# Seven-product up projections: h kept in fp32 for its combinations, made in three portions

## The chip, the cores and the metric

The kernel runs on one core of a Trainium2 chip. A core has TensorE (PE in the profile; PEld is its weight load), VectorE (DVE), ScalarE (ACT), GpSimd (POOL) and SyncE (SP), which here only issues transfers. The metric is the device time of one execution in microseconds, lower is better; the runs shown give a median.

## What is computed

A decoder trunk of two layers on 512 tokens of width 1024, all in fp32. Each layer is a half-step FFN, a token mixer and another half-step FFN, and each of the three starts with an adaptive norm:

```python
mod = cond @ ada_w[l] + ada_b[l]          # nine vectors: shift, scale, gate of three sub-layers
h = modulate(x, norm_ffn1[l], sh1, sc1)   # rms_norm(x) * gain * (1 + scale) + shift
x = x + 0.5 * (1.0 + g1)[:, None] * swiglu(h, ffn1_w1[l], ffn1_w3[l], ffn1_w2[l])
# swiglu(h, w1, w3, w2) = (silu(h @ w1) * (h @ w3)) @ w2, hidden width 2816
h = modulate(x, norm_mix[l], sh2, sc2)
x = x + (1.0 + g2)[:, None] * token_mix(h, ...)
h = modulate(x, norm_ffn2[l], sh3, sc3)
x = x + 0.5 * (1.0 + g3)[:, None] * swiglu(h, ffn2_w1[l], ffn2_w3[l], ffn2_w2[l])
```

The change touches the four FFNs (ffn1 and ffn2 of both layers), the norms ahead of them and the work of the conditioning.

## The kernel before

Activations lie feature-major: 128 features by 512 tokens, x as 8 such k-tiles. Every fp32 product is made of three passes over rounded parts: a factor is split into a high part (a cast, ACT) and a low part (value less high part, DVE), and `mm3` multiplies high by high, high by low and low by high. The normed h is kept only in parts, `hhi` and `hlo`. Weights come in slabs of 128 x 1024 (`slab`): SP issues the transfer into a `raw` buffer (there are 2), ACT casts the halves into `whi` (L120), DVE subtracts for `wlo` (L121); there are 3 buffers each of whi and wlo.

An FFN has 22 m-tiles of the hidden width. The first ones (4, or 6 in the very first FFN) are made plainly: `first` (or `first_begun`) and then `up(m)`, each with one slab of w1 and one of w3, and Silu and a product behind (`glu`: ACT L492, DVE L493). The others go in pairs of m-tiles (`pairs`) with seven block products in place of eight. For these h is cut into four blocks of 4 k-tiles by 256 tokens, b11, b12, b21, b22, and `fast_acts` makes four combinations of them, each split again into parts and kept in two tiles with the tag `A`: b11 - b12, then the negative of its sum with b22, then of that with b21, and b22 - b12 apart, which GpSimd computes. Since h is there in parts only, a difference takes three operations of 128 x 1024 and each further sum two; the running results take two of the five `L` buffers. `fast_acts` is called after the first `up(m)`. The pairs load their weight blocks into `raw` and `L`, two of them as a sum, where a second transfer, issued by GpSimd, adds to the first (L538).

After m-tiles 0 to 7, 8 to 15 and 16 to 21 comes a down projection each (`down`, through `close`), whose result is added to x (L388). The third close has more to do: its last four output tiles are made in two halves of 256 tokens, with the weights in the freed `A` tiles (`spare`), so that the norm of the next sub-layer can start on the first half while the second is multiplied. A norm sums squares (ACT L322, DVE L323), sums over partitions with PE, computes the inverse root on DVE, spreads it with PE, and then `norm_apply` makes h k-tile by k-tile: scaled on DVE (L378), high part with the shift on ACT (L379), low part on DVE (L384), or for k = 3, 5, 7 the full h on ACT (L381) and the low part on GpSimd (L382). In the first FFN of layer 0 `begin` does this in an order written out by hand; there L1479 and L1444 make hhi and hlo.

The conditioning (`mod`) is a product of a vector with 72 weight blocks a layer. `ada_block` loads one block of 512 KB into `L` (SP) and makes one DVE operation with it (L268). They wait in a queue, and `tick` takes one or more from it at set places: two after each `up(m)` past the first, two after each pair, one per output tile of a down projection. What is left is emitted by `drain` before the mixer.

The framework's planner puts each engine's instructions into their order: it follows the order of the code, but lets an instruction pass an earlier one that it reckons not ready; only those named to `keep_in_program_order` (the conditioning products, the beginning, the first half's norm on PE) keep theirs. Each engine and each transfer queue then works strictly in its planned order. Buffers are named by tags, with the counts in `BUFS` (`c3` 5, `cv` 3, `g` 7); a tile waits until an older one of its tag is done with.

Of the kernel before, what the change touches and what calls it, by code (L numbers as in the profile page):

```python
# [73 lines left out]
class Trunk:  # L74
    def __init__(self, ctx, tc, aps):
        self.tc = tc
        self.nc = tc.nc
        self.ap = aps
        self.sb = ctx.enter_context(tc.tile_pool(name="sb", bufs=1))
        self.ps = ctx.enter_context(tc.tile_pool(name="ps", bufs=1, space=bass.MemoryType.PSUM))  # L80
        self.count = 0
        self.pin = False
        self.units, self.body, self.ahead = [], None, None
        self.queue = []
        self.waiting = []

    def order(self, i):

        return self.tc.keep_in_program_order(i)
# [20 lines left out]
        return self.ps.tile(list(shape), F32, tag=tag, name=f"{tag}_{self.count}", bufs=BUFS[tag])  # L110


    def slab(self, src, n, place=None):
        nc = self.nc
        raw = self.t("raw", [P, 1024])
        hi, lo = place or (self.t("whi", [P, 1024], F32R), self.t("wlo", [P, 1024], F32R))
        nc.sync.dma_start(raw[:, :n], src)
        for a in range(0, n, 512):
            s = slice(a, min(a + 512, n))
            nc.scalar.copy(hi[:, s], raw[:, s])  # L120
            nc.vector.tensor_sub(lo[:, s], raw[:, s], hi[:, s].bitcast(F32))  # L121
        return hi, lo
# [7 lines left out]
    def split(self, hi, lo, src, scale=None):  # L130

        nc = self.nc
        if scale is None:
            nc.scalar.copy(hi, src)
            nc.vector.tensor_sub(lo, src, hi.bitcast(F32))  # L135
        else:
            nc.scalar.activation(hi, src, AF.Identity, scale=scale)
            nc.vector.scalar_tensor_tensor(lo, src, scale, hi.bitcast(F32), ALU.mult, ALU.subtract)
# [229 lines left out]
    def norm_apply(self, j, gain, mod, cols, rb):  # L368
        nc = self.nc
        a, b = cols  # L370
        if a == 0:
            self.hhi = self.t("hhi", [P, KT, SEQ], F32R)
            self.hlo = self.t("hlo", [P, KT, SEQ], F32R)
        for k in range(KT):
            h = self.t("g", [P, SEQ])
            sh = mod[:, 3 * j * KT + k:3 * j * KT + k + 1]
            hi, lo = self.hhi[:, k, a:b], self.hlo[:, k, a:b]
            nc.vector.scalar_tensor_tensor(h[:, a:b], self.x[:, k, a:b], gain[:, k:k + 1], rb, ALU.mult, ALU.mult)  # L378
            nc.scalar.activation(hi, h[:, a:b], AF.Identity, bias=sh)  # L379
            if k in (3, 5, 7):  # L380
                nc.scalar.activation(h[:, a:b], h[:, a:b], AF.Identity, bias=sh)  # L381
                nc.gpsimd.tensor_sub(lo, h[:, a:b], hi.bitcast(F32))  # L382
            else:
                nc.vector.scalar_tensor_tensor(lo, h[:, a:b], sh, hi.bitcast(F32), ALU.add, ALU.subtract)  # L384

    def residual(self, m, ps, gate, cols):
        a, b = cols
        self.nc.vector.scalar_tensor_tensor(self.x[:, m, a:b], ps[:, a:b], gate[:, m:m + 1], self.x[:, m, a:b],  # L388
                                            ALU.mult, ALU.add)

    def close(self, get, acts, gate, finish, spare=(), ahead=None):

        late = KT - len(spare)
        for m in range(late):
            s = get(m)
            ps = self.p("acc")
            self.proj(ps, s, acts)
            self.residual(m, ps, gate, FULL[0])
            if finish is not None:
                finish(m, FULL[0])  # L400
            self.tick()
        ws = [get(m, place) for m, place in zip(range(late, KT), spare)]
        if ahead is not None:
            ahead()
        self.tick(len(ws))
        norms = []
        for (a, b), tag in zip(HALVES if ws else (), ("acc", "sc")):
            for m, s in zip(range(late, KT), ws):
                ps = self.p(tag)
                n = len(acts)  # L410

                cut = NORM_AT.get(m - late, n) if norms else n
                self.proj(ps, s, acts, (a, b), range(cut))
# [14 lines left out]
        return [self.slab(self.ap[f"{w}_{n}"][l, m].rearrange("p k c -> p (k c)"), 1024)  # L428
                for n, m in (("w1", 0), ("w3", 0), ("w1", 1))]

    def fast_acts(self):


        nc = self.nc

        def quarter(i, j):
            return [t[:, 4 * i:4 * i + 4, j * 256:(j + 1) * 256] for t in (self.hhi, self.hlo)]

        f32 = lambda t: t.bitcast(F32)
        b11, b12, b21, b22 = (quarter(i, j) for i in range(2) for j in range(2))  # L440
        store = [self.t("A", [P, 4, 4, 256], F32R) for _ in range(2)]
        places = [(st[:, i], st[:, i + 1]) for st in store for i in (0, 2)]
        new = lambda: self.t("L", [P, 4, 256])

        def difference(a, b, eng):
            t = new()
            eng.tensor_sub(t, f32(a[0]), f32(b[0]))
            eng.tensor_add(t, t, f32(a[1]))
            eng.tensor_sub(t, t, f32(b[1]))
            return t  # L450

        def minus_sum(a, b):

            nc.vector.scalar_tensor_tensor(a, a, -1.0, f32(b[0]), ALU.mult, ALU.subtract)
            nc.vector.tensor_sub(a, a, f32(b[1]))

        def split(place, t):
            nc.scalar.copy(place[0], t)
            nc.vector.tensor_sub(place[1], t, f32(place[0]))

        t = difference(b11, b12, nc.vector)
        split(places[0], t)
        t3 = difference(b22, b12, nc.gpsimd)
        minus_sum(t, b22)
        split(places[1], t)
        minus_sum(t, b21)
        split(places[3], t)
        split(places[2], t3)
        return [b11, places[0], places[1], b21, places[2], b22, places[3]]

    def ffn(self, l, w, gate, finish, early, ahead=None):

        nc = self.nc
        w1, w3, w2, w13 = (self.ap[f"{w}_{n}"] for n in ("w1", "w3", "w2", "w13"))
        acts = self.hacts()
        g = {}
# [185 lines left out]
        def down(i):  # L662
            k0, k1 = THIRDS[i]
            xs = [g[k] for k in range(k0, k1)]
            get = lambda m, place=None: self.slab(w2[l, m, :, k0:k1, :].rearrange("p k c -> p (k c)"), (k1 - k0) * P,
                                                  place)
            spare = []
            if i == 2:
                for _ in range(2):
                    sp = self.t("A", [P, 4, 1024], F32R)  # L670
                    spare += [(sp[:, 0], sp[:, 1]), (sp[:, 2], sp[:, 3])]
            self.close(get, xs, gate, finish if i == 2 else None, spare, ahead if i == 2 else None)

        begun = len(early) > 3
        plain = 6 if begun else 4
        m = first_begun() if begun else first()
        comb = None
        while m < plain:
            up(m)
            m += 1  # L680
            if comb is None:
                comb = self.fast_acts()
        pairs(range(plain, 10, 2), comb)
        down(0)
        pairs(range(10, 18, 2), comb)
        down(1)
        pairs(range(18, FT, 2), comb)
        down(2)


# [946 lines left out]
```

## Time and profile before

| | |
|---|---|
| median of 3 runs | 2803.44 us (2800.72 to 2805.31) |
| the profiled execution | 2798.02 us |
| its span, first to last instruction | 2796.3 us |
| mean granted TensorE clock | 0.991 |
| instructions | 44477 |

The profile gives, for one execution, the busy time of each engine, the chain of work that ended last, groups of instructions by line, and who waited for whom. A row of a group names the line, the engine, the operation, the tile written and those read, and the shape. A row of the waits names the waiting instruction's engine, tile and line and what released it. Line numbers are those of the kernel before. Matmuls overlap, so that PE's busy time contains stretches in which it is not at its full pace.

### The profile page before, as it was taken

What the parts mean: (1) busy time and instruction counts of PE and PEld (TensorE: products, weight loads), DVE (VectorE), ACT (ScalarE), POOL (GpSimd) and SP (SyncE); (2) the same over time, 40 slices, a digit from 0 to 9 for tenths busy, and PEclk for the clock granted to TensorE, in tenths of its full rate; (3) what the DMA queues carried; (4) which work ended last, traced back from release to release, by engine and by line L of the source; (5) the groups of instructions that cost most, each with busy time, mean ns of one, the idle gap of its engine ahead of it and who ended that gap; (6) DMA issues with size and microseconds to landing.
All of it is one profiled execution on the core that took longest, in us unless ns stands there. A gap on an engine that the chain in (4) does not pass through costs nothing.

```text
span 2796.3 us, 44477 instructions
## 1 busy us (share of the span) xinstructions
PE 2711.5 (97%) x17168; PEld 2406.5 (86%) x17168; DVE 2048.5 (73%) x3978; ACT 1288.0 (46%) x2494; POOL 350.3 (13%) x429
## 2 busy tenths in 40 slices
PE   7999989999999998999999999999999999989999
PEld 6889977788888787999979999887888888979988
DVE  7868788767668767776678787887766786676655
ACT  4535345444446434443535344445444564344533
POOL 1001014100001012011021010150000111121100
PEclk9999999999999999999999999999999999999999
DMA  7677753222122344776337776432222223356542
GB/s 265 203 211 229 209 166 106 87 80 80 59 85 69 125 147 128 225 202 199 110 96 209 208 237 200 155 102 91 73 83 72 77 79 117 128 158 204 151 129 90
DMA packets 118868, 394.65 MB, mean 141 GB/s; under 512 B 13440, under 2 KB 16128, under 8 KB 118656
## 3 DMA queue, kind: packets, MB, share of 16 engines
q1 hardware_dynamic: 106128, 350.38, 37.7%
q0 software_dynamic: 10080, 36.70, 7.4%
q10 hardware_dynamic: 2448, 4.72, 0.4%
q8 instruction: 135, 2.21, 0.3%
q14 instruction: 77, 0.63, 0.1%
HBM read 376.55 MB, written 15.20 MB: 140 GB/s over the span
## 4 chain that ended last, share of the span: by engine, by line
PE 74%; DVE 14%; DMA 5%; ACT 3%; issue 2%; POOL 2%; SPq 0%; ACTq 0%; DVEq 0%; POOLq 0%
PE acc L93 52%; PE sc L93 14%; PE sm L93 4%; DMA raw<-in_ffn_w 3%; DVE wlo L121 2%; PE sm L98 2%; DVE L L268 1%; PE po L93 1%; DVE cv L699 1%; ACT whi L120 1%; DVE g L378 1%; DVE L L831 1%; DVE L L833 1%; DVE hlo L384 1%; DMA raw<-in_w_in 0%
## 5 line engine op out<-in xcount | busy, mean ns | idle before, releaser
L93 PE MATMUL acc<-hhi,whi 128*128 128x512 f32 (+1 forms) x1368 | 506.3, 371 | 11.4 <-DVE cv L699 7.4
L120 ACT CAST whi<-raw 128x512 fp32r<-128x512 f32 (+2 forms) x554 | 320.8, 606 | 400.1 <-PE acc L93 309.2
L93 PE MATMUL acc<-hlo,whi 128*128 128x512 f32 (+1 forms) x1368 | 487.2, 356 | 4.9 <-POOL hlo L382 3.9
L93 PE MATMUL acc<-hhi,wlo 128*128 128x512 f32 (+1 forms) x1368 | 486.4, 356 | 0.0
L93 PE MATMUL acc<-O,whi 128*128 128x512 f32 x1472 | 454.6, 390 | 0.0
L121 DVE TENSOR_TENSOR wlo<-raw,whi 128x512 fp32r<-128x512 f32 (+2 forms) x554 | 395.9, 732 | 76.7 <-ACT whi L120 69.4
L93 PE MATMUL acc<-A,whi 128*128 128x256 f32 (+1 forms) x1808 | 348.3, 292 | 4.7 <-ACT cv L647 4.7
L93 PEld LDWEIGHTS acc<-O,whi 128*128 128x128 f32 x1472 | 275.1, 188 | 56.8 <-DVE O L135 0.8
L93 PEld LDWEIGHTS acc<-A,whi 128*128 128x128 f32 x1808 | 287.0, 192 | 11.0 <-ACT cv L647 5.7
L93 PEld LDWEIGHTS acc<-hhi,whi 128*128 128x128 f32 x1368 | 259.3, 190 | 42.6 <-issue 10.1
L93 PEld LDWEIGHTS acc<-hhi,wlo 128*128 128x128 f32 x1368 | 259.0, 189 | 38.2 <-DVE wlo L121 0.9
L93 PEld LDWEIGHTS acc<-hlo,whi 128*128 128x128 f32 x1368 | 260.0, 190 | 35.8 <-POOL hlo L382 7.3
L93 PE MATMUL acc<-O,wlo 128*128 128x512 f32 x736 | 286.6, 389 | 0.0
L93 PE MATMUL acc<-A,wlo 128*128 128x256 f32 (+1 forms) x904 | 263.3, 291 | 0.0
L561 DVE TENSOR_TENSOR wlo<-raw,whi 128x1024 fp32r<-128x1024 f32 x140 | 171.0, 1222 | 92.0 <-ACT whi L560 87.3
L560 ACT CAST whi<-raw 128x1024 fp32r<-128x1024 f32 x140 | 146.5, 1047 | 190.9 <-PE acc L93 101.7
L388 DVE SCALAR_TENSOR_TENSOR M<-acc,gate,M 128x512 f32<-128x512 f32 (+1 forms) x112 | 77.3, 691 | 148.7 <-PE acc L93 148.5
L93 PEld LDWEIGHTS acc<-A,wlo 128*128 128x128 f32 x904 | 173.9, 192 | 2.5
L268 DVE SCALAR_TENSOR_TENSOR L<-L,kph 128x1024 f32<-128x1024 f32 x142 | 171.0, 1227 | 0.0
L560 ACT CAST whi<-L 128x1024 fp32r<-128x1024 f32 x105 | 110.0, 1048 | 131.8 <-PE acc L93 35.1
L93 PEld LDWEIGHTS acc<-O,wlo 128*128 128x128 f32 x736 | 138.2, 188 | 28.7
L93 PE MATMUL sc<-hhi,whi 128*128 128x256 f32 (+1 forms) x432 | 138.6, 321 | 12.6 <-ACT whi L120 8.7
(417 smaller groups left out, 5453.8 us busy)
## 6 DMA issues: line engine op xcount, KB each, us to landing
raw<-in_ffn_w SPq DMA_DIRECT2D x166, 512.0 KB, 4.5
L<-in_ada_w SPq DMA_DIRECT2D x142, 512.0 KB, 4.8
raw<-in_w_in SPq DMA_DIRECT2D x108, 512.0 KB, 3.4
L<-in_ffn_w SPq DMA_DIRECT2D x105, 512.0 KB, 4.7
L<-in_ffn_w POOLq DMA_DIRECT2D x70, 512.0 KB, 7.6
raw<-in_ffn_w SPq DMA_DIRECT2D x32, 384.0 KB, 3.2
raw<-in_w_branch_a SPq DMA_DIRECT2D x16, 512.0 KB, 3.5
raw<-in_w_branch_b SPq DMA_DIRECT2D x16, 512.0 KB, 3.4
```

What stands on the lines that cost most here:

```text
L93: i = self.nc.tensor.matmul(*a, **k)
L98: i = self.nc.tensor.transpose(*a, **k)
L120: nc.scalar.copy(hi[:, s], raw[:, s])
L121: nc.vector.tensor_sub(lo[:, s], raw[:, s], hi[:, s].bitcast(F32))
L268: self.order(self.nc.vector.scalar_tensor_tensor(raw, raw, 1.0, self.condb, ALU.mult, ALU.mult, accum_out=mod[:, o:o + 1]))
L378: nc.vector.scalar_tensor_tensor(h[:, a:b], self.x[:, k, a:b], gain[:, k:k + 1], rb, ALU.mult, ALU.mult)
L384: nc.vector.scalar_tensor_tensor(lo, h[:, a:b], sh, hi.bitcast(F32), ALU.add, ALU.subtract)
L388: self.nc.vector.scalar_tensor_tensor(self.x[:, m, a:b], ps[:, a:b], gate[:, m:m + 1], self.x[:, m, a:b], ALU.mult, ALU.add)
L560: nc.scalar.copy(hi, t)
L561: nc.vector.tensor_sub(lo, t, hi[:].bitcast(F32))
L699: nc.vector.scalar_tensor_tensor(acc[:, s:], ps[:, :SEQ - s], w[j], acc[:, s:], ALU.mult, ALU.add)
L831: nc.vector.tensor_mul(tv, f[:, j + 1:, j:j + 1].to_broadcast([P, n, w]), x[:, j:j + 1, :w].to_broadcast([P, n, w]))
```

## The change

- `norm_apply` keeps h in fp32 for the norms ahead of an FFN (j = 0 and 2): it writes h into eight tiles of 128 x 2 x 256, called quarters, five with the tag `c3` and three with the tag `cv`, in place of `g`. For k = 3, 5, 7 h gets its shift as before; for the other five an activation is added after the loop.
- `fast_acts` works in place on the quarters, with one operation per sum and tile of 512 columns. It is now a generator of three portions: the first is asked for before the first `up(m)`, the others after one `up(m)` each. In the first FFN, where `begin` has kept no h, GpSimd first adds hi and lo into the quarters.
- `slab` can load into another tag; the weights of the third close's last four tiles go through `L` in place of `raw`.
- `close` takes numbers of ticks: two and one in turn in the first and second down projection of an FFN, none in the third. Before it was one per tile in all three.

```diff
-        raw = self.t("raw", [P, 1024])
+        raw = self.t(home, [P, 1024])
...
+        keep = j != 1
+        late = []
         for k in range(KT):
-            h = self.t("g", [P, SEQ])
+            if not keep:
+                h = self.t("g", [P, SEQ])[:, a:b]
+            elif k % 2 == 0:
+                q = self.quarter(k // 2, a // 256)
+            if keep:
+                h = q[:, k % 2, :]
...
             else:
-                nc.vector.scalar_tensor_tensor(lo, h[:, a:b], sh, hi.bitcast(F32), ALU.add, ALU.subtract)
+                nc.vector.scalar_tensor_tensor(lo, h, sh, hi.bitcast(F32), ALU.add, ALU.subtract)
+                late.append((h, sh))
+        for h, sh in late if keep else ():
+            nc.scalar.activation(h, h, AF.Identity, bias=sh)
+
+    def quarter(self, i, half):
+        n = len(self.quarters)
+        q = self.quarters[i, half] = self.t("c3" if n < 5 else "cv", [P, 2, 256])
+        return q
...
-    def close(self, get, acts, gate, finish, spare=(), ahead=None):
+    def close(self, get, acts, gate, finish, spare=(), ahead=None, ticks=(1, 1)):
...
-            self.tick()
+            self.tick(ticks[m % 2])
...
-        self.tick(len(ws))
+        self.tick(ticks[0] * len(ws))
...
-    def fast_acts(self):
+    def fast_acts(self, comb):
...
+        if not self.quarters:
+            for j in range(2):
+                for i in range(4):
+                    hi, lo = (t[:, 2 * i:2 * i + 2, j * 256:(j + 1) * 256].bitcast(F32) for t in (self.hhi, self.hlo))
+                    nc.gpsimd.tensor_add(self.quarter(i, j), hi, lo)
+        b11, b12, b21, b22 = ([self.quarters[2 * i + n, j] for n in range(2)] for i in range(2) for j in range(2))
...
         def split(place, t):
-            nc.scalar.copy(place[0], t)
-            nc.vector.tensor_sub(place[1], t, f32(place[0]))
-        t = difference(b11, b12, nc.vector)
-        split(places[0], t)
-        t3 = difference(b22, b12, nc.gpsimd)
-        minus_sum(t, b22)
-        split(places[1], t)
-        minus_sum(t, b21)
-        split(places[3], t)
-        split(places[2], t3)
+            for n in range(2):
+                hi, lo = (p[:, 2 * n:2 * n + 2, :] for p in place)
+                nc.scalar.copy(hi, t[n])
+                nc.vector.tensor_sub(lo, t[n], hi.bitcast(F32))
+        def minus_sum(t, b):
+            for n in range(2):
+                nc.vector.scalar_tensor_tensor(t[n], t[n], -1.0, b[n], ALU.mult, ALU.subtract)
+        for n in range(2):
+            nc.vector.tensor_sub(b11[n], b11[n], b12[n])
+        for n in range(2):
+            nc.gpsimd.tensor_sub(b12[n], b22[n], b12[n])
+        split(places[0], b11)
+        yield
+        minus_sum(b11, b22)
+        split(places[1], b11)
+        yield
+        split(places[2], b12)
+        minus_sum(b11, b21)
+        split(places[3], b11)
+        yield
...
-                                                  place)
+                                                  place, "L" if place else "raw")
...
-            self.close(get, xs, gate, finish if i == 2 else None, spare, ahead if i == 2 else None)
+            self.close(get, xs, gate, finish if i == 2 else None, spare, ahead if i == 2 else None,
+                       (0, 0) if i == 2 else (2, 1))
...
-        comb = None
+        comb = []
+        make = self.fast_acts(comb)
+        next(make)
         while m < plain:
             up(m)
             m += 1
-            if comb is None:
-                comb = self.fast_acts()
+            next(make, None)
```

More of the change, by code (lines that the diff above doesn't have):

```diff
@@ L85, in __init__ @@
         self.waiting = []
+        self.quarters = {}
     def order(self, i):
@@ L110, in p, with slab @@
         return self.ps.tile(list(shape), F32, tag=tag, name=f"{tag}_{self.count}", bufs=BUFS[tag])
-    def slab(self, src, n, place=None):
+    def slab(self, src, n, place=None, home="raw"):
         nc = self.nc
-        raw = self.t("raw", [P, 1024])
+        raw = self.t(home, [P, 1024])
         hi, lo = place or (self.t("whi", [P, 1024], F32R), self.t("wlo", [P, 1024], F32R))
@@ L373, in norm_apply @@
             self.hlo = self.t("hlo", [P, KT, SEQ], F32R)
+            self.quarters = {}
+        keep = j != 1
+        late = []
         for k in range(KT):
-            h = self.t("g", [P, SEQ])
+            if not keep:
[4 more added lines that the diff above has]
+                h = q[:, k % 2, :]
             sh = mod[:, 3 * j * KT + k:3 * j * KT + k + 1]
             hi, lo = self.hhi[:, k, a:b], self.hlo[:, k, a:b]
-            nc.vector.scalar_tensor_tensor(h[:, a:b], self.x[:, k, a:b], gain[:, k:k + 1], rb, ALU.mult, ALU.mult)
-            nc.scalar.activation(hi, h[:, a:b], AF.Identity, bias=sh)
+            nc.vector.scalar_tensor_tensor(h, self.x[:, k, a:b], gain[:, k:k + 1], rb, ALU.mult, ALU.mult)
+            nc.scalar.activation(hi, h, AF.Identity, bias=sh)
             if k in (3, 5, 7):
-                nc.scalar.activation(h[:, a:b], h[:, a:b], AF.Identity, bias=sh)
-                nc.gpsimd.tensor_sub(lo, h[:, a:b], hi.bitcast(F32))
-            else:
-                nc.vector.scalar_tensor_tensor(lo, h[:, a:b], sh, hi.bitcast(F32), ALU.add, ALU.subtract)
+                nc.scalar.activation(h, h, AF.Identity, bias=sh)
+                nc.gpsimd.tensor_sub(lo, h, hi.bitcast(F32))
+            else:
+                nc.vector.scalar_tensor_tensor(lo, h, sh, hi.bitcast(F32), ALU.add, ALU.subtract)
+                late.append((h, sh))
+        for h, sh in late if keep else ():
+            nc.scalar.activation(h, h, AF.Identity, bias=sh)
+    def quarter(self, i, half):
+        n = len(self.quarters)
+        q = self.quarters[i, half] = self.t("c3" if n < 5 else "cv", [P, 2, 256])
+        return q
     def residual(self, m, ps, gate, cols):
@@ L429, in ffn_early, with parts @@
                 for n, m in (("w1", 0), ("w3", 0), ("w1", 1))]
-    def fast_acts(self):
+    def fast_acts(self, comb):
         nc = self.nc
-        def quarter(i, j):
+        def parts(i, j):
             return [t[:, 4 * i:4 * i + 4, j * 256:(j + 1) * 256] for t in (self.hhi, self.hlo)]
-        f32 = lambda t: t.bitcast(F32)
-        b11, b12, b21, b22 = (quarter(i, j) for i in range(2) for j in range(2))
+        if not self.quarters:
[4 more added lines that the diff above has]
+        b11, b12, b21, b22 = ([self.quarters[2 * i + n, j] for n in range(2)] for i in range(2) for j in range(2))
@@ L441, in fast_acts @@
         store = [self.t("A", [P, 4, 4, 256], F32R) for _ in range(2)]
         places = [(st[:, i], st[:, i + 1]) for st in store for i in (0, 2)]
[L443 to L455, printed above, removed]
@@ L457, in split @@
-        def split(place, t):
-            nc.scalar.copy(place[0], t)
-            nc.vector.tensor_sub(place[1], t, f32(place[0]))
-        t = difference(b11, b12, nc.vector)
-        split(places[0], t)
-        t3 = difference(b22, b12, nc.gpsimd)
-        minus_sum(t, b22)
-        split(places[1], t)
-        minus_sum(t, b21)
-        split(places[3], t)
-        split(places[2], t3)
-        return [b11, places[0], places[1], b21, places[2], b22, places[3]]
+        comb += [parts(0, 0), places[0], places[1], parts(1, 0), places[2], parts(1, 1), places[3]]
```

## The prediction

> **What bounds the kernel now.** I read the page first, then who the TensorE waits for, then the stretches in which it waits, engine by engine.
>
> ```profile
> PE 2711.5 (97%) x17168; PEld 2406.5 (86%) x17168; DVE 2048.5 (73%) x3978; ACT 1288.0 (46%) x2494; POOL 350.3 (13%) x429
> PE 74%; DVE 14%; DMA 5%; ACT 3%; issue 2%; POOL 2%; SPq 0%; ACTq 0%; DVEq 0%; POOLq 0%
> ```
>
> PE is busy for 97% of the span and makes up 74% of the chain that ended last. The change takes no matmul away, so it can win only time in which PE waits. The second view lists those waits: the waiting instruction, what released it, microseconds in total, how often, the longest.
>
> ```profile
> PE sc L93 <- DVE wlo L121: 8.9, 3, 3.1
> PE sc L93 <- ACT whi L120: 8.7, 3, 3.4
> PE sc L93 <- DVE M L388: 7.6, 2, 3.8
> ...
> PE acc L93 <- ACT cv L647: 4.7, 5, 2.7
> PE acc L93 <- POOL hlo L382: 3.9, 3, 1.3
> PE sc L93 <- DVE g L493: 3.9, 1, 3.9
> PE acc L93 <- DVE M L388: 2.5, 2, 1.8
> ...
> PE acc L93 <- ACT hhi L379: 2.2, 2, 1.1
> ...
> PE sc L93 <- ACT whi L560: 1.0, 1, 1.0
> ...
> PE sc L93 <- DVE wlo L561: 0.8, 1, 0.8
> ```
>
> Three rows come three times each: they sit where the last three FFNs begin (near 1066, 1430 and 2451 us). Two L388 rows and L379 come twice: the closes of the two ffn1. L493 comes once, in the first FFN. The L560 and L561 rows are the first pair of layer 1's ffn1. All of these lie in stretches that the change rewrites.
>
> Now the start of layer 0's ffn2, engine by engine (start, duration, operation; in brackets the idle time before it).
>
> ```profile
> 1070.79 0.80 PE L93 MATMUL sc<-hhi,whi 128*128 128x512 f32 x1 [3.36 <-ACT whi L120]
> ...
> 1075.08 0.79 PE L93 MATMUL sc<-hhi,wlo 128*128 128x512 f32 x1 [3.07 <-DVE wlo L121]
> ```
>
> ```profile
> 1062.16 3.42 DVE L448 TENSOR_TENSOR L<-L,hlo 128x1024 f32<-128x1024 f32 x1
> 1065.68 1.56 DVE L449 TENSOR_TENSOR L<-L,hlo 128x1024 f32<-128x1024 f32 x1
> 1068.35 2.18 DVE L459 TENSOR_TENSOR A<-L,A 128x1024 fp32r<-128x1024 f32 x1 [1.11 <-ACT A L458]
> 1070.56 3.26 DVE L454 SCALAR_TENSOR_TENSOR L<-L,hhi 128x1024 f32<-128x1024 f32 x1
> 1073.74 0.67 DVE L493 TENSOR_TENSOR g<-g,sc 128x512 f32<-128x512 f32 x1
> 1074.34 1.28 DVE L121 TENSOR_TENSOR wlo<-raw,whi 128x512 fp32r<-128x512 f32 x2
> ...
> 1085.31 1.22 DVE L454 SCALAR_TENSOR_TENSOR L<-L,hhi 128x1024 f32<-128x1024 f32 x1
> ```
>
> ```profile
> 1061.91 2.58 POOL L447 TENSOR_TENSOR L<-hhi 128x1024 f32<-128x1024 f32 x1
> 1064.45 1.70 POOL L382 TENSOR_TENSOR hlo<-g,hhi 128x256 fp32r<-128x256 f32 x1
> 1066.23 3.21 POOL L448 TENSOR_TENSOR L<-L,hlo 128x1024 f32<-128x1024 f32 x1
> 1069.52 3.22 POOL L449 TENSOR_TENSOR L<-L,hlo 128x1024 f32<-128x1024 f32 x1
> ```
>
> ```profile
> 1067.27 1.04 ACT L458 CAST A<-L 128x1024 fp32r<-128x1024 f32 x1 [5.63 <-DVE L L449]
> 1068.34 1.28 ACT L492 ACT_TABLE_LOAD   x1
> 1069.63 0.60 ACT L492 ACTIVATE g<-acc 128x512 f32<-128x512 f32 x1
> 1070.12 1.13 ACT L120 CAST whi<-raw 128x512 fp32r<-128x512 f32 x2
> ```
>
> The combinations of h (L447 to L459), written in the code behind the first up(m), run ahead of the weights of the m-tile before it. ACT sits behind the cast L458, which waits 5.63 us for DVE's L449; then come table load and Silu, and only then the weights' cast. DVE's own queue is slow because it alternates with POOL: L454 takes 3.26 us beside POOL's L449 and 1.22 us later, alone. POOL's L447 also stands ahead of the last low half of h (L382), for which PE waits 1.3 us.
>
> The close of layer 0's ffn1:
>
> ```profile
> 383.06 1.22 DVE L268 SCALAR_TENSOR_TENSOR L<-L,kph 128x1024 f32<-128x1024 f32 x1
> ...
> 386.49 1.22 DVE L268 SCALAR_TENSOR_TENSOR L<-L,kph 128x1024 f32<-128x1024 f32 x1
> ...
> 388.05 0.47 DVE L388 SCALAR_TENSOR_TENSOR M<-sc,gate,M 128x256 f32<-128x256 f32 x1
> ```
>
> Four conditioning products, 383.06 to 387.64, stand in front of the residual that frees a PSUM bank; PE waits 3.8 us for it, in each ffn1.
>
> **The change part by part.**
>
> *A. Conditioning out of the third down projection, its last weights through L.* Eight products per ffn1 move to the first two downs; the number of ticks stays the same (8+8+8 becomes 12+12+0), so as many as now are left for the drain. In the close goes 7.6 (L388, sc) + 2.5 (L388, acc) + 2.2 (L379: the norm, now run late behind those products) = 12.3 us over both ffn1. The four raw loads through L no longer wait for two raw buffers. Late next is the norm's own chain. I take 11 of 12.3, since the products left to the drain may slip into DVE's gaps; bounds 7.6 (only the sc waits) and 12.3. The other FFNs have no such waits and win nothing.
>
> *B. The first m-tiles of the last three FFNs.* The waits sum to 8.9 + 8.7 + 3.9 = 21.5 us. DVE's work before the weights shrinks: a difference was three 1024-wide operations (3 x 1.22 alone, 3.42 and 1.56 in place), now two of 512 columns (0.67 each, as L493); a minus-sum two of 1024, now two of 512. POOL's three operations (2.58 + 3.21 + 3.22 = 9.0 us) become two of 512 columns:
>
> ```profile
> L648 POOL TENSOR_TENSOR cv<-cv,cv x35: 1286/1774/1842, 117.5 to 2754.1; 128x512 f32<-128x512 f32 x35
> L382 POOL TENSOR_TENSOR hlo<-g,hhi x30: 737/754/1704, 397.9 to 2449.6; 128x256 fp32r<-128x256 f32 x30
> ```
>
> (minimum/median/maximum ns): 2.6 to 3.7 us. They need h with its shift of k = 6 and 7, so they come behind the last L382, which then takes its 0.75 us, and the 3.9 us go. What is left is serial: the weights' high buffer is free only when its last matmul is done, then ACT 0.6, DVE 0.7 and a Silu of 0.6 between; some 2 us per FFN. I count 6 us left of 21.5.
>
> Added are five activations per half (h with its shift, for k = 0, 1, 2, 4, 6) of 128x256:
>
> ```profile
> L381 ACT ACTIVATE g<-g,mod 128x256 f32<-128x256 f32 x30 | 14.9, 497 | 0.3
> ...
> 1050.38 0.40 ACT L322 ACTIVATE g<-M 128x256 f32<-128x256 f32 x1
> ...
> 1050.69 0.49 ACT L381 ACTIVATE g<-g,mod 128x256 f32<-128x256 f32 x1
> ...
> 1055.77 1.31 ACT L379 ACTIVATE hhi<-g,mod 128x256 fp32r<-128x256 f32 x3 [4.58 <-DVE g L378]
> ```
>
> Back to back, 0.40 us each. In the second half they are covered by PE's 8.6 us of first products. In the first half ACT has gaps for three; two may stand before the square L322 at 1050.38, which starts the second half's norm, on whose result (hhi at 1055.77) PE arrives without slack. That costs 0 to 1.2 us; I take 0.5 per FFN, 1.5 in all. So B gives 21.5 - 6 - 1.5 = 14. Bounds: 3.9 (only L382's wait goes) and 21.5.
>
> *C. The first FFN.* No h is kept there: eight POOL additions of 128x512 make it from hi and lo, plus two subtractions, against three operations now.
>
> ```profile
> 56.72 2.56 POOL L447 TENSOR_TENSOR L<-hhi 128x1024 f32<-128x1024 f32 x1 [56.27 <-ACT hhi L1479]
> ...
> 63.29 3.27 POOL L449 TENSOR_TENSOR L<-L,hlo 128x1024 f32<-128x1024 f32 x1
> ```
>
> ```profile
> L1444 DVE SCALAR_TENSOR_TENSOR hlo<-g,mod,hhi x8: 744/748/2895, 20.0 to 56.9; 128x512 fp32r<-128x512 f32 x8
> ```
>
> POOL is idle for the 56 us before, and most additions can start when their two k-tiles are ready. But the longest L1444, 2895 ns against 748, ran beside POOL's L447: additions among DVE's pinned chain delay it. PE works off seven products there without a wait, which covers some microseconds. Now it waits 3.9 us for L493. I take a gain of 1.5; bounds +3.9 gained and 6 lost (ten operations of 1.3 to 1.8 us, 13 to 18, less today's 9.1, with part of it exposed).
>
> [...]
>
> *D. L freed earlier.* fast_acts held two of five L buffers until its last L459; f1 of the first pair waits for one. PE's 1.0 + 0.8 us and the 2.7 us behind L647 follow in layer 1's ffn1. I take 2 us; bounds 0 and 4.5. Holding c3 and cv until the third portion delays nobody: their first users (p5, place(8)) come with the pairs, after it.
>
> *E. Twelve conditioning loads per down instead of eight.* A row of windows: time, PE, DVE, ACT, POOL busy, clock, DMA share, GB/s.
>
> ```profile
> 138.00:188.00 50.00, 50.00 (x248) 42.51 (x248) 34.74 (x56) 13.55 (x23) 3.32 (x5) 1.00 0.73 223
> ```
>
> DVE gets 4 x 1.23 us more in 50 us, 34.7 to 39.6: still hidden. The queue on SP gets 4 x 0.52 MB more, 223 to some 265 GB/s, which by the share of 0.73 would be 0.87. PE waits nowhere there now and five slabs are on the way, so I take 0; it can't gain. At the other end each of 40 m-tiles could lose something (third rival).
>
> **Sum.** 11 + 14 + 1.5 + 2 = 28.5 us. The profiled execution took 2798.02 us with a span of 2796.3, so it would take 2769.5. The runs shown have a median of 2803.44, 5.4 above it; the forecast is for the median: 2775.
>
> **The rivals.** *1. The serial chain stays.* The portions still run ahead of the first weights on ACT and DVE, as they do now, and a shorter wait in front is followed by a longer one behind. For it: L458 and L454 stand before L121 though written later. Against it: DVE's wait there is the alternation with POOL, and POOL's part falls from 9.0 to 3.7 us at most. B then gives 3.9 and less the 1.5: 11 + 2.4 + 0 + 1 = 14, so 2789.
>
> *2. Nothing to measure.* The close waits as before, for the conditioning left to the drain, and the first FFN loses 6 us to POOL's additions: 14 + 0 + 2 - 6 = 10 less late loads in the downs, 2798 to 2803. The close speaks against it: those products are written before its last m-tiles now, and would not be then.
>
> *3. Slower: the downs become bound by transfers.* Two m-tiles there then move 2 slabs and 3 conditioning blocks, 2.6 MB in 2 x 5.45 us of PE. If the transfers held only some 200 GB/s, each m-tile would lose 1.1 us, 40 of them 44 us: 2775 + 44 = 2819. It decides once an m-tile loses 0.85 us (0.85 x 40 = 34 us eats the gain and 0.2%), that is, under 208 GB/s. The row above holds 223 at a share of 0.73, so I give it little.
>
> **How the numbers follow.** The forecast (2762 to 2784) has 6.5 in 10, the first rival 2 in 10, the second 0.8, the third 0.7. The range runs from 2760 (nearly all bounds on the good side: 12.3 + 21.5 + 3.9 + 4.5 = 42.2 gives 2761) to 2797, which takes in the first rival and the mishaps of C. 0.2% is 5.6 us, about what a measurement of this kernel tells from no change: faster 0.86, same 0.07, slower 0.07.
>
> **What would show it.** A: no four L268 before an L388 in the ffn1 closes, PE's L388 and L379 waits gone. B: the three L120/L121 waits down to about 2 us together per FFN, no L382 wait; POOL's operations there under 1.9 us. C: no wait above 3 us at 68 us. D: no L560 wait near 1470 us. E: no wait on L120 in the downs. The forecast is wrong if PE waits for hhi in the middle of the first products by more than 1.5 us (late activations), if the first FFN's DVE chain pushes PE into waits before 60 us, or if ACT waits for raw in the downs.

## The result, and the profile after

The changed kernel takes 2782.12 us (median of 4 runs, 2778.55 to 2787.33); the kernel before, on the same chip, 2802.08 us. The ratio is 0.9929, interval 0.9908 to 0.995: 20 us won where 28.5 were forecast. The profiled execution took 2779.66 us, with a span of 2777.9 (18.4 less than before) and a mean granted clock of 0.995 (0.991 before). Line numbers have moved: by one up to the norm, by 10 where the norm makes h, by 19 in the close, by 21 in the pairs, by 23 in the beginning of the first FFN.

First the list of what TensorE waits for, in the changed kernel (waiting instruction, releaser, total, how often, longest).

```profile
PE acc L94 <- ACT cv L668: 7.8, 8, 2.4
PE sc L94 <- DVE g L514: 7.4, 1, 7.4
PE sc L94 <- DVE wlo L582: 7.4, 5, 2.8
...
PE sc L94 <- ACT whi L121: 3.4, 3, 1.1
PE acc L94 <- ACT hhi L389: 2.9, 3, 1.1
...
PE sc L94 <- DVE wlo L122: 1.4, 3, 0.5
```

The 8.7 + 8.9 us for the first weights of the last three FFNs have become 3.4 + 1.4; the 3.9 for POOL's low half and the residual's 7.6 in the closes are gone. Two rows speak against the forecast: g (L514, the first FFN) has gone from 3.9 to 7.4 us, and wlo of the pairs (L582) from 0.8 to 7.4.

Both programs issue 17168 matmuls, in nearly the same order, so the starts of the nth matmul in the two traces give a ledger by place (worked out from the traces, us of span, minus is won):

| place | term | measured | forecast |
|---|---|---|---|
| the two closes of ffn1 | A | -9.9, -7.9 | -11 |
| starts of the last three FFNs | B | -9.4, -6.2, -9.7; late activations +1.2, +1.1, +1.1 | -14 net |
| first FFN's start | C | +5.2 | -1.5 |
| first pair of layer 1's ffn1 | D | -7.1 | -2 |
| the pairs and downs: ffn1 l0, ffn2 l0, ffn1 l1 | E | +9.9, +2.3, +9.3 | 0 |
| all else | | +1.7 | 0 |

The sum is -18.4. So 47 us were won where the waits had been and 27 paid at two places that the forecast had put at a gain of 1.5 and at 0; it came out near only since the errors are of opposite sign, which is luck. Of the first 9.9, 1.7 lie at 125 us, ahead of the first down, so that some 20 of E's 21.5 lie behind the downs. One ledger is one execution: in the other trace of the changed kernel (c1 below) A (9.9 and 7.9) and D (7.1) are the same, C is 4.7, and E is 8.9, 3.5 and 2.8.

**Where more was won than waited.** The waits that A took away add up to 12.3 us, yet the closes won 17.8. B's waits fell by 16.7 and its three places won 25.3. Windows show why (time, then PE, PEld, DVE, ACT, POOL busy, granted clock, DMA share, GB/s): the first close, the start of ffn2 of layer 0, and the first FFN, before and then after.

```profile
384.00:400.00 16.00, 11.01 (x67) 10.10 (x67) 12.97 (x39) 5.59 (x14) 1.50 (x2) 0.79 0.58 201
1068.00:1084.00 16.00, 10.15 (x30) 7.63 (x31) 13.63 (x13) 9.80 (x16) 4.66 (x2) 0.68 0.32 100
...
60.00:90.00 30.00, 26.08 (x108) 21.07 (x107) 25.47 (x28) 15.41 (x24) 6.48 (x2) 0.94 0.31 95
```

```profile
384.00:400.00 16.00, 15.98 (x134) 15.77 (x133) 10.45 (x31) 5.02 (x12) 0.00 (x0) 1.00 0.38 127
1068.00:1084.00 16.00, 14.31 (x81) 12.31 (x82) 15.91 (x22) 12.70 (x24) 5.02 (x5) 1.00 0.21 67
...
60.00:90.00 30.00, 22.64 (x88) 18.12 (x87) 22.50 (x34) 14.46 (x26) 8.03 (x6) 0.83 0.40 112
```

In each of these stretches that holds a long wait the granted clock is 0.68 to 0.94, and in the two where the wait is gone it is 1.00. The first FFN after, matmul by matmul, shows the size:

```profile
68.33 0.39 PE L94 MATMUL sm<-hhi,O 128*128 128x512 f32 x1
76.07 0.79 PE L94 MATMUL sc<-hhi,whi 128*128 128x512 f32 x1 [7.36 <-DVE g L514]
76.66 0.63 PE L94 MATMUL sc<-hlo,whi 128*128 128x512 f32 x1
77.09 0.63 PE L94 MATMUL sc<-hhi,wlo 128*128 128x512 f32 x1
...
81.36 0.63 PE L94 MATMUL sc<-hhi,whi 128*128 128x512 f32 x1
81.78 0.48 PE L94 MATMUL sc<-hlo,whi 128*128 128x512 f32 x1
82.11 0.39 PE L94 MATMUL sc<-hhi,wlo 128*128 128x512 f32 x1
82.33 0.39 PE L94 MATMUL sc<-hhi,whi 128*128 128x512 f32 x1
```

Behind 7.36 us of standing still the matmuls start 0.43 us apart, until 81.8; then 0.23 us apart. From 76.07 to 81.78 there are 13 of them: 13 x 0.2 = 2.6 us on top of the wait. The granted clock in the trace is 0.50 from 71.7 to 82.0 us, from within the wait on, and 1.00 just before and behind: half the clock, and about half the pace (0.43 against 0.23 us). Of that stretch 5.7 us hold slow matmuls.

**Where it was paid: the first FFN.** POOL, then DVE, then ACT, after.

```profile
53.09 2.20 POOL L462 TENSOR_TENSOR c<-hhi,hlo 128x512 f32<-128x512 f32 x1 [10.02 <-DVE hlo L1467]
55.26 1.34 POOL L462 TENSOR_TENSOR cv<-hhi,hlo 128x512 f32<-128x512 f32 x1
62.79 2.53 POOL L462 TENSOR_TENSOR c<-hhi,hlo 128x512 f32<-128x512 f32 x2 [6.19 <-DVE hlo L1467]
```

```profile
61.96 0.75 DVE L1467 SCALAR_TENSOR_TENSOR hlo<-g,mod,hhi 128x512 fp32r<-128x512 f32 x1 [0.79 <-ACT hhi L1502]
65.35 1.76 DVE L479 TENSOR_TENSOR c<-c,c 128x512 f32<-128x512 f32 x1 [2.64 <-POOL c L462]
```

```profile
71.73 0.62 ACT L471 CAST A<-c 128x512 fp32r<-128x512 f32 x1 [2.26 <-DVE c L476]
72.26 1.13 ACT L121 CAST whi<-raw 128x512 fp32r<-128x512 f32 x2
73.41 1.28 ACT L513 ACT_TABLE_LOAD   x1
```

POOL stands still until the last k-tile's low half is there (62.7), since each addition takes two k-tiles; only behind its additions can b11 - b12 begin, at 65.35. From there a chain of DVE and ACT, each waiting for the other, leads to the Silu (74.70), the product L514 and the matmul at 76.07.

**Where it was paid: behind the downs.** DVE, after the first down of layer 0.

```profile
191.09 1.23 DVE L588 TENSOR_TENSOR raw<-raw,L 128x1024 f32<-128x1024 f32 x1 [7.04 <-DMA L<-in_ffn_w]
192.24 0.74 DVE L407 SCALAR_TENSOR_TENSOR M<-acc,gate,M 128x512 f32<-128x512 f32 x1
192.90 1.22 DVE L269 SCALAR_TENSOR_TENSOR L<-L,kph 128x1024 f32<-128x1024 f32 x1
...
194.04 1.22 DVE L269 SCALAR_TENSOR_TENSOR L<-L,kph 128x1024 f32<-128x1024 f32 x1
...
195.18 1.22 DVE L582 TENSOR_TENSOR wlo<-L,whi 128x1024 fp32r<-128x1024 f32 x1
```

Before, the same addition ran without a wait:

```profile
177.23 1.23 DVE L567 TENSOR_TENSOR raw<-raw,L 128x1024 f32<-128x1024 f32 x1
```

Now it waits 7.04 us for its load; behind it on DVE stand the residual and two conditioning products, and only then the weights' low half, for which PE waits 1.49 us. Behind the second down it is 8.34 us, in layer 1 7.62 and 6.98. Why the load is late stands in SP's waits between 160 and 200 us, after:

```profile
SPq L554 <- DVE L L269: 16.3, 5, 10.8
SPq L267 <- DVE L L269: 11.1, 5, 3.9
```

SP's queue issues the pair's load (L554) only when a conditioning product (L269) has freed one of the five L buffers: once it took 10.8 us. Before, these waits were more in all (20.5 us) and the longest was 5.1; so it is the one at the down's end that counts, not their sum. Bytes are not what was short (time, PE, PEld, DVE, ACT, POOL busy, clock, DMA share, GB/s):

```profile
138.00:188.00 50.00, 50.00 (x262) 43.16 (x262) 36.34 (x59) 15.09 (x26) 3.04 (x3) 1.00 0.82 260
188.00:200.00 12.00, 10.51 (x73) 9.64 (x72) 8.91 (x12) 4.35 (x5) 0.00 (x0) 1.00 0.72 171
```

PE has no gap up to 188 us, and waits where the rate is low.

### The profile page after: what moved, and what is told of

Read it like the earlier page. It is cut to its first block, busy times and chain, and to the rows that moved or that the text cites. A ratio compares the mean times of both kernels' runs of the same rounds, so it can differ in the third digit from the quotient of the medians.

```text
span 2777.9 us, 44536 instructions
## 1 busy us (share of the span) xinstructions
PE 2705.7 (97%) x17168; PEld 2401.9 (86%) x17168; DVE 2023.3 (73%) x3990; ACT 1299.2 (47%) x2540; POOL 335.3 (12%) x433
## 4 chain that ended last, share of the span: by engine, by line
PE 73%; DVE 15%; DMA 5%; ACT 3%; issue 2%; POOL 2%; SPq 0%; ACTq 0%; POOLq 0%; DVEq 0%
PE acc L94 52%; PE sc L94 14%; PE sm L94 4%; DMA raw<-in_ffn_w 3%; PE sm L99 2%; DVE L L269 2%; DVE wlo L122 2%; PE po L94 1%; DMA L<-in_ffn_w 1%; DVE wlo L582 1%; DVE cv L722 1%; DVE L L854 1%; DVE L L856 1%; DMA raw<-in_w_out 1%; ACT whi L121 0%
## 5 line engine op out<-in xcount | busy, mean ns | idle before, releaser
L121 ACT CAST whi<-raw 128x512 fp32r<-128x512 f32 (+2 forms) x554 | 320.3, 606 | 395.0 <-PE acc L94 305.8
L122 DVE TENSOR_TENSOR wlo<-raw,whi 128x512 fp32r<-128x512 f32 (+2 forms) x554 | 393.8, 729 | 69.4 <-ACT whi L121 62.2
L582 DVE TENSOR_TENSOR wlo<-raw,whi 128x1024 fp32r<-128x1024 f32 x140 | 170.6, 1221 | 93.9 <-ACT whi L581 89.3
L407 DVE SCALAR_TENSOR_TENSOR M<-acc,gate,M 128x512 f32<-128x512 f32 (+1 forms) x112 | 77.5, 692 | 131.5 <-PE acc L94 124.3
L269 DVE SCALAR_TENSOR_TENSOR L<-L,kph 128x1024 f32<-128x1024 f32 x142 | 171.4, 1235 | 0.0
L559 POOL DMA_DIRECT2D L<-in_ffn_w x70 | 61.2, 875 | 729.7 <-DMA L<-in_ffn_w 257.4
```

The source lines that it names most:

```text
L269: self.order(self.nc.vector.scalar_tensor_tensor(raw, raw, 1.0, self.condb, ALU.mult, ALU.mult, accum_out=mod[:, o:o + 1]))
L559: nc.gpsimd.dma_start(t, w13[l, m2, half2].rearrange("p w k c -> p (w k c)"), accum_op=ALU.add)
L582: nc.vector.tensor_sub(lo, t, hi[:].bitcast(F32))
```

## The experiments

All ratios are against the kernel before, run on the same chip. The changed kernel itself, run once more beside e5 to e7, gave 2775.73 us, 0.9916 [0.9903, 0.993].

**Ticks as before.** In the changed kernel:

```
-                       (0, 0) if i == 2 else (2, 1))
+                       (1, 1))
```

> The changed kernel with the old ticks, one per output tile in all three down projections; all else stays changed. Theory: the conditioning put into the first two downs costs the changed kernel about 9 us, since the five L buffers are then still taken when the next pair's first blocks are to be loaded, and DVE waits for them with the residual and the weights behind it; and its leaving the third close won some 10 us (two waits of 3.8 us for a residual behind four products, and the late norm). Taking both back leaves the time about where it is: 2782 +- 4, with the waits on the pairs' wlo behind the downs gone (7.4 + 1.0 us in the changed kernel) and the 3.8 us residual waits back. Rival: the new waits behind the downs come from elsewhere (the fp32 quarters holding c3 and cv, or the order of the planner); then they stay, and the time rises by the close's 8 to 12 us, to 2790 to 2794.

2774.78 us, 0.9911 [0.9898, 0.9925]: the ratio is that of the changed kernel within the intervals, though the time lies under the 2782 +- 4 expected. Two rows rose (from 1.1 and 2.9 us in the changed kernel):

```profile
PE acc L94 <- DVE M L407: 5.7, 2, 3.2
PE acc L94 <- ACT hhi L389: 5.1, 5, 1.1
```

The closes wait for the residual again, and no wait for L582 is left. By the same matmuls against the kernel before, the closes win 0.9 and 3.0 us here (9.9 and 7.9 in the changed kernel), and the three stretches behind the downs lose nothing (0.0, -0.2, -1.3; there +8.3, +2.3, +9.3). So the moved conditioning lost behind the downs about what it won in the closes. The loss ahead of the first down stays (4.0 us with the old ticks, 1.7 with the new): it is not part of E.

**Part A alone, on the kernel before.** The parameter ticks with (0, 0) and (2, 1), and the last weights' home L; nothing else of the change.

> Only part A and with it E, put into the kernel before: conditioning (2, 1) per m-tile in the first two downs and none in the third, the last four m-tiles' weights through L. Theory (from the same matmuls' times in the two traces): the closes win 9.9 + 7.9 us, and behind the downs some 22 us are lost since the five L buffers hold conditioning when the next pair's block sums want to be loaded; net about +4, so 2800 to 2810 us, ratio 0.998 to 1.004. The waits for the residual (7.6 and 2.5 us) go, and the first addition of f1 behind a down waits 6 to 8 us for its load. Rival (the forecast's terms A and E): the closes win 11 and E costs nothing, 2791 us, ratio 0.996, with no such wait for a load.

2796.4 us, 0.9991 [0.9975, 1.0007], within the theory's ratio (not its 2800 to 2810 us) and against the forecast's 0.996. By the same matmuls the closes won 9.9 and 7.9 us. The stretches behind the downs lost some 13 of that again (7.0, 1.8 and 4.5), and the rest went before the first down (3.7) and at the first pair of layer 1's ffn1 (2.1). DVE's rows behind the first and second down:

```profile
190.20 1.23 DVE L567 TENSOR_TENSOR raw<-raw,L 128x1024 f32<-128x1024 f32 x1 [8.50 <-DMA L<-in_ffn_w]
...
318.07 1.23 DVE L567 TENSOR_TENSOR raw<-raw,L 128x1024 f32<-128x1024 f32 x1 [7.49 <-DMA L<-in_ffn_w]
```

So terms A and E are one edit, and its net here is nothing that can be measured.

**The last weights through raw again.**

```
-                                                  place, "L" if place else "raw")
+                                                  place)
```

> The changed kernel with the last four m-tiles' weights back in raw (two buffers) and the conditioning left where the change put it. Theory: what held the residual was the conditioning on VectorE, not the loads, so the closes stay as after: no wait for the residual over 1 us, 2771 to 2784 us, ratio 0.990 to 0.995; with two buffers of L less in use at the close nothing moves at the downs. Rival (the forecast's sentence that the loads no longer wait for two raw buffers): waits of 2 to 4 us come back in each of the two closes, 2778 to 2790 us.

2769.52 us, 0.9892 [0.9874, 0.991], a little under the time and ratio expected; no wait for the residual (L407) came back. What A won was mainly the conditioning taken out of the close. By the same matmuls the closes won 8.7 and 6.8 us, 2.3 less in all than with L as the home: small waits came up in the norm (0.6 and 0.5 us for L324). So L was worth those 2.3 us in the closes. Whether raw is the better home in the whole stays open, since the interval overlaps the changed kernel's.

**Twelve ticks early in the down.** As many products in each of the first two downs, but two at each of six m-tiles out of eight and none at the last two:

```
-            self.tick(ticks[m % 2])
+            self.tick(ticks[m % len(ticks)])
-                       (0, 0) if i == 2 else (2, 1))
+                       (0, 0) if i == 2 else (2, 2, 2, 2, 2, 2, 0, 0))
```

> The changed kernel with the twelve conditioning products of a down put into its first six output tiles (2,2,2,2,2,2,0,0) in place of 2 and 1 in turn; the same number and the same bytes. Theory (L buffers and DVE's queue at the end of a down): the pairs' first blocks find free L buffers, the waits on the pairs' wlo behind the downs fall from 8.4 us to under 2, and the time falls by 6 to 9 us to about 2774. Rival (too many bytes in the downs: 0.80 of the transfer engines' time and 243 GB/s there against 0.75 and 221 before): the same bytes in a shorter time make it no better, 2780 to 2788, and weights' casts in the downs begin to wait for raw.

2761.82 us, 0.9859 [0.9844, 0.9874], more won than expected (2774): 13 us less than the version with the old ticks on the same chip, whose ratio is that of the changed kernel. The waits for L582 are gone; the addition behind the first down, and the transfers up to it:

```profile
186.62 1.23 DVE L588 TENSOR_TENSOR raw<-raw,L 128x1024 f32<-128x1024 f32 x1 [2.66 <-DMA L<-in_ffn_w]
```

```profile
138.00:188.00 50.00, 50.00 (x258) 42.92 (x257) 39.98 (x66) 15.40 (x26) 3.03 (x3) 1.00 0.86 279
188.00:200.00 12.00, 12.00 (x92) 11.57 (x91) 7.30 (x7) 4.89 (x6) 1.75 (x2) 1.00 0.99 260
```

279 GB/s, more than the 260 of the changed kernel, and PE without a gap: more bytes in the same time and no loss there. The transfer rate in the down as the cause of E falls; the buffers and queue places held at its end remain, and how much is due to each was not tried apart. In this execution layer 0's ffn1 was not cured, however: PE, then ACT,

```profile
253.99 0.80 PE L94 MATMUL acc<-A,whi 128*128 128x256 f32 x2 [5.26 <-ACT cv L668]
252.41 1.04 ACT L581 CAST whi<-raw 128x1024 fp32r<-128x1024 f32 x1 [8.01 <-DMA raw<-in_ffn_w]
```

some 60 us behind the down a copy stands behind a cast whose load is late (245 to 255 us: a share of 0.91, 296 GB/s). By the same matmuls the three stretches lose 9.4, -1.1 and -0.4 us. In the combined version below, with the same ticks, that wait is absent and they lose 0.0, -0.8 and -0.9. The profiled execution is the longest of this run's four; why the load was late in it stays open.

**The first FFN's h from ACT.** begin writes h plus its shift, 128x256 at a time, into the tiles that POOL's eight additions had filled (an extract; the norm's factor there also goes to another tag):

```
+            for half in range(2):
+                if k % 2 == 0:
+                    self.quarter(k // 2, half)
+                nc.scalar.activation(self.quarters[k // 2, half][:, k % 2, :], h[:, half * 256:(half + 1) * 256],
+                                     AF.Identity, bias=sh)
```

> The changed kernel, but in the first FFN ScalarE writes h with its shift straight into the quarters (16 activations of 128x256), in place of GpSimd's eight additions of hi and lo; the factor of the norm there goes to another buffer tag. Theory: the additions cost the first FFN about 4 us against before (the wait for the first product of Silu and w3 rose from 3.9 to 7.4 us, and 0.6 us at 59 us), because the last three stand behind the last low half of h and the subtractions behind them, and because DVE alternates with them. Without them that wait falls under 3 us and the time by 4 to 7 us, to 2775 to 2778. Rival: the wait is set by the cast, the table load and Silu on ScalarE behind the end of the seven products, and 16 more activations there make it no better: 2781 to 2785.

2763.64 us, 0.9869 [0.9853, 0.9885], under the 2775 to 2778 expected. The wait for L514 is gone altogether, and with it the slow matmuls (this kernel, then the changed one, both from 66 to 88 us):

```profile
66.00:88.00 22.00, 22.00 (x99) 18.22 (x98) 15.49 (x25) 13.75 (x24) 0.00 (x0) 1.00 0.43 139
```

```profile
66.00:88.00 22.00, 14.64 (x52) 11.52 (x52) 19.07 (x27) 13.59 (x24) 4.82 (x4) 0.77 0.37 96
```

By the same matmuls this start won 10.3 us, for a wait of 7.4: more than expected, by the clock's share.

**The subtraction b22 - b12 on DVE.**

```
-            nc.gpsimd.tensor_sub(b12[n], b22[n], b12[n])
+            nc.vector.tensor_sub(b12[n], b22[n], b12[n])
```

> The changed kernel with b22 - b12 on VectorE in place of GpSimd. Theory (VectorE and GpSimd alternate on operations that read two tiles): VectorE's operations at the start of an FFN lose the 1 to 1.7 us that two or three of them take beside GpSimd's; the two subtractions cost it 1.3 us instead; the wait for the weights' cast at the three starts falls from 1.1 us each to about 0.5, and the first FFN's wait from 7.4 to 5 to 6 us; 2 to 4 us less in all. Rival: what is left there is the serial chain of cast, table load and Silu; no change, or 1 us more for VectorE's longer queue.

2770.88 us, 0.9907 [0.9891, 0.9922], no difference that can be told from the changed kernel (2 to 4 us were expected). The wait for L514 fell from 7.4 to 5.9 us, so POOL's two subtractions are the smaller part of it; e3 shows that the additions are the larger.

**The first half's late activations behind the square.** The list late of half 0 is kept and worked off at the start of half 1.

> The changed kernel, but the five added activations of the first half of h are emitted at the head of the second half's norm, so that they stand behind the square that starts it. Theory: the 0.9 us waits for hhi in the middle of the first products of ffn2 (two of them) and the 1.1 us one at the head of layer 1's ffn1 come from these activations standing ahead of that square; they go, 2 to 3 us in all: 2779 to 2780. Rival: ScalarE reaches the square in time and the waits are the norm's own chain through DVE and PE: no change, 2782, and the activations may now delay the second half's hhi instead, up to 2785.

2768.39 us, 0.9897 [0.988, 0.9914]. The row for hhi L389 (2.9 us, three times) is gone, as expected, but the waits for the copies into cv (L668 in the changed kernel) went from 7.8 to 11.3 us in this execution, and the interval overlaps the changed kernel's. That the late activations cause those three waits is shown, and by the same matmuls the three places, which lost 1.2, 1.1 and 1.1 us, lose nothing here; in the time of the whole kernel it can't be told.

**One portion instead of three.**

```
-        next(make)
         while m < plain:
             up(m)
             m += 1
-            next(make, None)
+            for _ in make:
+                pass
```

> The changed kernel with all three portions asked for after the first up(m), as the old kernel did, h in fp32 as in the change. Theory: the gain at the FFNs' starts comes from the shorter work (one operation per sum, two GpSimd operations of 1.4 to 1.7 us for three of 2.6 to 3.2), and the planner puts it ahead of the weights in either case: within 3 us of the changed kernel, with waits of 1.1 and 0.5 us at the three starts as there. Rival: the portions do it; then the waits at the three starts come back in part, to 3 us or more each, and the time rises by 5 to 15 us.

2772.33 us, 0.9911 [0.9895, 0.9928], and the rows at the starts of the last three FFNs are those of the changed kernel (whi 3.4, wlo 1.4). The portions are not what won B. What is left is the shorter work (h kept in fp32, two operations instead of three, POOL's part small); it was not taken apart further.

**Three of these together** (ticks early in the down, h from ACT, late activations held):

> The changed kernel with three alterations together: the twelve conditioning products in the first six tiles of a down, h of the first FFN written by ScalarE, and the first half's added activations behind the square. Theory: the three costs are separate places and add up: 12 to 14 us (waits behind the downs) + 10 (first FFN) + 3 (late activations) under the changed kernel, a span near 2752 and a ratio to before of 0.983. Rival: one takes the other's gain, as the transfers move together once PE runs earlier; then no better than the best alone, 0.986.

2743.34 us, 0.9806 [0.9792, 0.982]; 32 us under the changed kernel on the same chip (2775.73), and more than expected. No wait for g of L514, wlo of L582 or hhi of L389 (lines of the changed kernel) is left, and the mean granted clock is 1.000.

**That, with b22 - b12 on DVE.**

> The combined version with b22 minus b12 on VectorE instead of GpSimd. Theory: GpSimd's two subtractions slow VectorE's operations beside them in each FFN (1.22 to 2.3 us and more), but in the combined version no TensorE wait hangs on them: 2739 to 2746 us, ratio 0.979 to 0.982. Rival (what it gave in the changed kernel, some 4.5 us between single runs, adds up like the others): 2738 us, ratio 0.9785.

2740.71 us, 0.9789 [0.9774, 0.9805]: the lowest time of all, but its interval overlaps that of the version without it. The row for whi L121 (3.4 us, three times) is gone; that for wlo L122 went from 1.4 to 2.1.

**Waits put in.** To the combined version, at the start of the last three FFNs:

```
+            for _ in range(again if a == 0 else 0):
+                nc.vector.tensor_sub(lo[:, s], raw[:, s], hi[:, s].bitcast(F32))
             nc.vector.tensor_sub(lo[:, s], raw[:, s], hi[:, s].bitcast(F32))
```

with again = 4, 8 and 16 for the weights of the third up projection there (w3, m = 1).

> The combined version with waits put in: at the start of the last three FFNs, ahead of the low half of one weight tile, VectorE repeats one 128x512 subtraction 4, 8 and 16 times (0.64 us each): 2.6, 5.1 and 10.2 us more for TensorE to wait, the same result. Theory of the clock (TensorE stands still, and then runs its next matmuls at about 0.43 us instead of 0.235): the two longer waits cost their length and 2 to 3 us beside it, so 17.9 + 4 to 6 us, about 2765 to 2768 us, and the windows behind them show a granted clock near 0.5 while that behind the shortest shows 1.00. Rival: a wait costs its length, 2761 us or less where VectorE's queue has slack, and the rate behind it is as everywhere.

2766.57 us, 0.9883 [0.9868, 0.9898]; by the spans of the two traces 21.3 us more than the combined version, which ran on another chip. The time lies in the range expected, but by another sum: the graded waits missed. The order of the work shifted around the repeats, TensorE took other matmuls first, and its waits there came out at 5.2, 4.5 and 5.2 us, so that no short one is left to compare with. What follows the second of them:

```profile
1413.49 0.50 PE L94 MATMUL sc<-hhi,whi 128*128 128x512 f32 x1 [1.13 <-ACT whi L121]
1413.83 0.40 PE L94 MATMUL sc<-hlo,whi 128*128 128x512 f32 x1
1415.50 0.50 PE L94 MATMUL acc<-hhi,whi 128*128 128x512 f32 x1 [1.28 <-ACT whi L121]
1415.84 0.40 PE L94 MATMUL acc<-hlo,whi 128*128 128x512 f32 x1
1418.29 0.79 PE L94 MATMUL acc<-hhi,wlo 128*128 128x512 f32 x1 [2.06 <-DVE wlo L124]
1418.88 0.63 PE L94 MATMUL acc<-hhi,whi 128*128 128x512 f32 x1
...
1423.57 0.52 PE L94 MATMUL acc<-hhi,wlo 128*128 128x512 f32 x1
1423.93 0.39 PE L94 MATMUL acc<-hhi,whi 128*128 128x512 f32 x1
```

By the same matmuls against the combined version the three starts lost 7.1, 5.7 and 6.7 us, 19.5 together. The waits there rose by 3.6, 2.9 and 3.6 (10.1; the 0.45 for wlo that it has at each was taken off). The other 9.4 us, 2.8 to 3.5 at each start, are matmuls at the slow rate. So the price of such a wait is its length and some 3 us behind it, shown by putting it in. A further wait of 1.53 us at 2440.8, behind the third start, is not counted; as much was won back soon after.

## Why the prediction was right in the sum and wrong in two steps

- **A, 11 forecast, 17.8 measured.** The mechanism holds: with no conditioning in the third down no four L268 stand before the residual, and both waits went; e1 brings them back. The term was mis-sized: it counted the waits' length and left out the slow matmuls behind them (17.8 - 12.3 = 5.5, two closes). The 17.8 lies over the upper bound of 12.3. The raw loads that no longer wait for two buffers were a small part of it: 2.3 us (e9).
- **B, 14 forecast, 21.9 measured.** 4.8 us of waits were left of 21.5, near the 6 counted. The rest of the difference is again the clock: 25.3 won for 16.7 of waits less (21.9 net of the late activations, just over the bound of 21.5). The late activations cost 3.4 instead of 1.5, at the waits for hhi that the forecast had named, and none above the 1.5 us that it gave as its limit.
- **C, 1.5 gained forecast, 5.2 lost.** The failed step is "PE works off seven products there without a wait, which covers some microseconds". It is not POOL's sum of work that counts but when its last additions can start: behind the last hlo, at 62.79, with three of them and all DVE and ACT steps still to come. The bound (6 lost) held. The rows show that DVE slows beside POOL (L479 takes 1.76 us at 65.35, beside L462, and 0.86 at 1067.73, beside POOL for a part of it). How much is that and how much POOL's own place in the chain, for which L479 waits 2.64 us, the runs do not separate: e6 took 1.5 us off the wait, and e3, which takes away both for the additions, all of it.
- **D, 2 forecast, 7.1 measured**, above the bound of 4.5. The L560, L561 and L647 waits there (1.0 + 0.8 + 2.7 us) are all gone, which is the bound. Of the other 2.6 us most is the clock: 0.88 in the 14 us from 1486 to 1500 before, 1.00 after, which is worth an estimated 14 x 0.12 = 1.7 us.
- **E, "five slabs are on the way, so I take 0": wrong, 21.5 lost by the ledger, some 20 of it behind the downs.** The window by which it was judged held busy shares and GB/s, and both came out near what was worked out (260 against 265 GB/s, DVE 36.3 against 39.6 us, PE without a gap). What was not in it: who holds the five L buffers at the end of the down, and what stands on DVE behind an addition whose load is late. The third rival was near in place (the loss came behind the downs, not in them) and had the mechanism wrong: e2 moves more bytes in the down and PE has no gap there, and the combined version, with as many products, loses nothing behind them.
- **The rivals.** The first (the chain stays) had the order right and the price wrong. At the start of layer 0's ffn2 the combinations still run ahead of the weights, after:

```profile
1074.02 1.28 DVE L476 SCALAR_TENSOR_TENSOR c<-c,cv 128x512 f32<-128x512 f32 x2
1075.22 0.68 DVE L122 TENSOR_TENSOR wlo<-raw,whi 128x512 fp32r<-128x512 f32 x1
```

  But PE now waits 1.13 + 0.46 us there in place of 3.36 + 3.07: the work is shorter, its order the same, which agrees with e7. The second had the first FFN's loss right and the close wrong. The third's 44 us did not come; half of it did, by another way.

## What to carry to other kernels

Price a wait of the TensorE at its length and the slow matmuls behind it: in this kernel some 1.7 to 3.5 us more at the places measured, where its waits came to 2.7 to 7.7 us in all. When work is moved into a stretch with room, ask not only whether the engines and the transfers have room, but which buffers the moved work still holds when the next stage wants them, and what stands in order behind the instruction that will wait; spacing the same work earlier won 13 us here. Where an engine prepares operands for a stage, look at when its last input arrives, not at how long it was idle before.

## What the runs showed of the hardware that was not expected

- Matmuls behind a long wait start 0.43 us apart instead of 0.23, for some 3 us (before, from 73.56) to nearly 8 us (e10, from 1057.6), and the granted clock of a window of 16 to 30 us around it falls to 0.68 to 0.94. In the granted clock of the two traces, before and after, every stretch at 0.50 that begins between 40 us and the last matmul lasts 3.4 us (as before from 73.4 and after from 450.6), 6.8 us (before from 387.5, after from 324.3) or 10.2 us (as before from 1070.1 and after from 71.7); the 10.2 us of the changed kernel's first FFN begin at 71.7, while TensorE still stands. The waits ahead of slow matmuls need not be in one piece: in e10 they were 1.13, 1.28 and 2.06 us with two matmuls between them. In the changed kernel 1.12 and 0.45 us at the start of layer 1's ffn1 had such matmuls behind them (granted clock 0.50 from 1433.6 to 1437.1), while 1.13 and 0.46 us at 1074.76 had none; how long a wait must be for it is not shown.
- The 16 DMA engines held a share of 0.99 at 260 GB/s over 12 us without making TensorE wait (e2, 188 to 200 us); the changed kernel, at 171 GB/s, waited there. The lower rate was the sign of the late issues, not their cause.
